# A two-level Strassen MLP: the 15-sum form, sums chained in PSUM, and a second level in the first matmul

What was changed: the outer products of a tuned MLP kernel go over from the 18-sum to the 15-sum form of a seven-product scheme (two ways to write it, with 18 or 15 sums of blocks around the seven products), their sums are chained in PSUM, the operands over g are made in place, products 2 and 3 of the first matmul get a second level, and x is cast before it is transposed.

## The chip, the cores and the metric

The kernel runs on one core of one Trainium2 chip. The metric is the device time of one launch in microseconds (us), the median of several runs. A profile of one execution is taken beside the timed runs; its "span", from the first to the last instruction, is some 1.8 us shorter than that execution's time. The granted TensorE clock, as a share of full speed, is given where it matters.

PE is TensorE's matmul side, PEld its weight loads, DVE is VectorE, ACT is ScalarE, POOL is GpSimd, SP is SyncE, whose queue (SPq) issues most loads.

## The reference

```python
x: (8, 1024, 1024)   w1: (1024, 4096)   w2: (4096, 1024)      # float32, normal draws
h = x @ w1
h = 0.5 * h * (1 + np.tanh(np.sqrt(2 / np.pi) * (h + 0.044715 * h ** 3)))
out = (h @ w2).astype(np.float32)
```

The kernel computes in float16 with float32 sums.

## The kernel before

The 8192 rows of x are worked on in eight row blocks of 1024 rows, numbered 0 to 7 here (`sb` in the code). For each one, "matmul 1" makes g = gelu(x w1) and "matmul 2" makes g w2. Both see their operands as 2 x 2 blocks and make seven block products instead of eight. Matmul 2 of row blocks 2 to 7 does so on two levels: each of the seven products is again seven smaller ones, of 256 columns. Matmul 1 has one level only, with matmuls of 512 columns. In row blocks 0 and 1 the operands made from w1 and w2 are made for the first time and stored in DRAM; later row blocks load them.

Matmul 1 before, for one chunk `c` of 128 rows of g (cut):

```python
pb, qb = psum(), psum()
product(pb, w, 4, True, False)          # four matmuls of 512 columns
v = temp()
nc.scalar.copy(out=v, in_=pb)
product(qb, w, 5, True, False)
u = temp()
tt(u, v, qb, SUB)                       # tt: a VectorE tensor_tensor
...
rb = psum()
product(rb, w, 1, True, False)
s = temp()
tt(s, u, rb, ADD)
product(pb, w, 2, False, True)
gelu("21", c, pb)
s2 = temp()
tt(s2, s, pb, SUB)
product(qb, w, 3, False, False)
gelu("12", c, qb)
product(rb, w, 7, False, True)
c11 = temp()
tt(c11, u, rb, ADD)
gelu("11", c, c11)
late = (c, w, qb, s2)                   # product 6 and g22: in the next chunk
```

That is five VectorE sums of 128x512 per chunk. In matmul 2 of row block 0 the first results leave PSUM through VectorE:

```python
for q, ps in product2(g, 4, pieces(4), pb, True, True):
    u[q] = temp()
    nc.vector.tensor_copy(out=u[q], in_=ps)
bring(("22",), late_copy, True)         # load w2's blocks and cast them on ScalarE
bring(("12",), late_copy, True)
```

The inner sums of w2 that row blocks 2 to 7 load are made on the way, some of them in matmul 1 of row blocks 1 and 2, half of those on GpSimd (`split_in_m1`, cut).

## Time and profile before

The median was 1513.1 us of 3 runs (1511.92 to 1513.27). What matters of the profile:

| | us |
|---|---|
| span | 1510.3 |
| start and matmul 1 of row block 0, until matmul 2 begins | 119.16 |
| matmul 2 of row block 0 | 96.70 |
| matmul 1 of row block 1 | 98.65 |
| matmul 2 of row block 1 | 96.69 |
| row blocks 2 to 7, to the end | 1099.1 |
| of that, one matmul 1 / one matmul 2 | 96.69 / 85.59 |

The page of the kernel before, its first line and the busy times of the engines:

```profile
span 1510.3 us, 24616 instructions
## 1 busy us (share of the span) xinstructions
PE 1499.5 (99%) x9278; PEld 908.6 (60%) x9278; DVE 1136.3 (75%) x1442; ACT 527.8 (35%) x958; POOL 409.4 (27%) x368
```

PE is busy 99% of the span, so a step that does not shorten PE's work, or its few gaps, gains nothing. The chain of work that ended last, kernel before (start in us, length in us, what):

```profile
411.37 96.82 PE ps L358 x448
508.19 85.59 PE ps L738 x784
593.77 96.69 PE ps L358 x448
```

One block of matmuls follows another with nothing between them. 96.69 us over 448 matmuls is 215.8 ns for 512 columns, and 85.59 us over 784 is 109.2 ns for 256. The four largest waits of PE in the whole run of the kernel before (waiting engine, line and tile; releaser; us in total, times, longest us):

```profile
PE ps L358 <- DVE tmp L144: 2.6, 4, 1.6
PE ps L358 <- DVE u L144: 1.5, 1, 1.5
PE ps L287 <- DVE warm L895: 1.2, 1, 1.2
PE ps L738 <- DVE u L144: 0.4, 1, 0.4
```

And the busy time of the engines in one later matmul 1 and one later matmul 2, kernel before:

```profile
core 0: us, PE busy (x) PEld busy (x) DVE busy (x) ACT busy (x) POOL busy (x), PEclk, DMA share, GB/s
593.61:690.30 96.69, 96.69 (x450) 43.83 (x448) 55.80 (x80) 46.29 (x79) 35.48 (x21) 1.00 0.84 253
508.20:593.80 85.60, 85.60 (x785) 76.65 (x784) 81.35 (x95) 18.26 (x43) 10.90 (x12) 1.00 1.00 337
```

VectorE, with 81.35 of 85.60 us, is nearly full in matmul 2, although PE waits for it there only once in the whole run, for 0.4 us.

### The profile page before, as it was taken

What the parts mean: (1) busy time and instruction counts of PE and PEld (TensorE: products, weight loads), DVE (VectorE), ACT (ScalarE), POOL (GpSimd) and SP (SyncE); (2) the same over time, 40 slices, a digit from 0 to 9 for tenths busy, and PEclk for the clock granted to TensorE, in tenths of its full rate; (3) what the DMA queues carried; (4) which work ended last, traced back from release to release, by engine and by line L of the source; (5) the groups of instructions that cost most, each with busy time, mean ns of one, the idle gap of its engine ahead of it and who ended that gap; (6) DMA issues with size and microseconds to landing.
All of it is one profiled execution on the core that took longest, in us unless ns stands there. A gap on an engine that the chain in (4) does not pass through costs nothing.

```text
span 1510.3 us, 24616 instructions
## 1 busy us (share of the span) xinstructions
PE 1499.5 (99%) x9278; PEld 908.6 (60%) x9278; DVE 1136.3 (75%) x1442; ACT 527.8 (35%) x958; POOL 409.4 (27%) x368
## 2 busy tenths in 40 slices
PE   9999999999999999999999999999999999999998
PEld 4444444444444687447864488644885458844687
DVE  5876868877755799558985589755996568965798
ACT  6655014420044322443234422344224442244321
POOL 1242022211379302170121601234112431105101
PEclk9999999999999999999999999999999999999999
DMA  9999877995899899968998899987999879994697
GB/s 319 341 342 363 241 269 279 337 357 176 318 372 251 302 317 347 311 164 313 318 320 282 201 327 323 302 252 204 358 315 310 237 220 337 312 365 147 211 324 240
DMA packets 235191, 438.92 MB, mean 291 GB/s; under 512 B 79552, under 2 KB 86720, under 8 KB 234176
## 3 DMA queue, kind: packets, MB, share of 16 engines
q1 hardware_dynamic: 205056, 337.71, 65.5%
q0 software_dynamic: 30016, 99.63, 23.0%
q8 instruction: 73, 1.20, 0.3%
q14 instruction: 46, 0.38, 0.1%
HBM read 334.50 MB, written 117.44 MB: 299 GB/s over the span
## 4 chain that ended last, share of the span: by engine, by line
PE 83%; DMA 1%; DVE 0%; issue 0%; DVEq 0%
PE ps L358 43%; PE ps L738 34%; PE ps L789 6%; DMA u<-raw_d 1%; DVE u L144 0%; DVE tmp L144 0%; DVEq L144 0%
## 5 line engine op out<-in xcount | busy, mean ns | idle before, releaser
L358 PE MATMUL ps<-u 128*128 128x512 f16 x3584 | 777.1, 379 | 4.3 <-DVE tmp L144 2.6
L358 PEld LDWEIGHTS <-u 128*128 128x128 f16 x3584 | 350.5, 98 | 428.6 <-issue 7.0
L144 DVE TENSOR_TENSOR tmp<-tmp,ps 128x512 f32<-128x512 f32 x528 | 362.2, 687 | 282.2 <-ACT tmp L422 109.7
L738 PE MATMUL ps<-u,gc 128*128 128x256 f16 x2688 | 300.4, 273 | 0.4 <-DVE u L144 0.4
L738 PEld LDWEIGHTS <-gc 128*128 128x128 f16 x2688 | 263.0, 98 | 31.2 <-issue 0.6
L368 ACT ACTIVATE g<-tmp 128x512 f16<-128x512 f32 x256 | 161.0, 631 | 287.2 <-DVE tmp L144 287.0
L144 DVE TENSOR_TENSOR u<-u 128x512 f32<-128x512 f32 (+3 forms) x278 | 239.5, 897 | 15.3 <-ACT u L313 12.4
L160 ACT COPY u<-ps 128x512 f32<-128x512 f32 x164 | 96.2, 586 | 390.2 <-PE ps L738 390.2
L492 POOL DMA_DIRECT2D out_dram<-u x80 | 76.3, 1090 | 556.6 <-DVE u L144 275.5
L368 ACT ACTIVATE g<-ps 128x512 f16<-128x512 f32 x256 | 152.1, 596 | 100.4 <-PE ps L358 100.3
L144 DVE TENSOR_TENSOR u<-u,ps 128x512 f32<-128x512 f32 x188 | 128.4, 683 | 32.7 <-PE ps L789 17.2
L789 PE MATMUL ps<-u,gc 128*128 128x512 f16 x640 | 138.8, 379 | 0.0
L738 PE MATMUL ps<-u,g 128*128 128x256 f16 x1152 | 132.6, 273 | 0.0
L738 PEld LDWEIGHTS <-g 128*128 128x128 f16 x1152 | 112.7, 98 | 14.3
L468 POOL TENSOR_TENSOR u<-g,g 128x2048 f16<-128x2048 f16 x24 | 97.0, 4064 | 44.7 <-ACT g L368 44.7
L789 PEld LDWEIGHTS <-gc 128*128 128x128 f16 x640 | 62.6, 98 | 75.5
L738 PE MATMUL ps<-u 128*128 128x256 f16 x864 | 99.2, 273 | 0.0
L144 DVE TENSOR_TENSOR tmp<-ps,tmp 128x512 f32<-128x512 f32 x128 | 88.4, 690 | 13.1 <-PE ps L358 8.5
L738 PEld LDWEIGHTS <-u 128*128 128x128 f16 x864 | 84.6, 98 | 9.8
L422 ACT COPY tmp<-ps 128x512 f32<-128x512 f32 x128 | 73.0, 570 | 36.1 <-PE ps L358 36.1
L144 DVE TENSOR_TENSOR u<-g,g 128x2048 f16<-128x2048 f16 x48 | 57.9, 1222 | 9.0 <-PE ps L738 9.0
L144 DVE TENSOR_TENSOR gc<-g,gc 128x2048 f16<-128x2048 f16 x48 | 58.6, 1220 | 1.0 <-ACT g L368 1.0
(43 smaller groups left out, 664.5 us busy)
## 6 DMA issues: line engine op xcount, KB each, us to landing
u<-w_d SPq DMA_DIRECT2D x420, 256.0 KB, 6.7
u<-in_d SPq DMA_DIRECT2D x168, 512.0 KB, 7.4
u<-raw_d SPq DMA_DIRECT2D x168, 256.0 KB, 6.4
out_dram<-u POOLq DMA_DIRECT2D x80, 512.0 KB, 10.5
gc<-in_w_dram SPq DMA_DIRECT2D x48, 512.0 KB, 5.6
w_d<-u POOLq DMA_DIRECT2D x36, 512.0 KB, 6.0
raw_d<-u SPq DMA_DIRECT2D x32, 512.0 KB, 10.7
u<-raw_d SPq DMA_DIRECT2D x32, 512.0 KB, 11.5
```

What stands on the lines that cost most here:

```text
L144: i = nc.vector.tensor_tensor(out=out, in0=in0, in1=in1, op=op)
L160: tc.keep_in_program_order(nc.scalar.copy(out=out, in_=in_))
L358: nc.tensor.matmul(bank, lhsT=ops[:, k, :], rhs=xs[m][:, k, :], start=(first and k == 0), stop=(k == KH - 1), skip_group_check=not first,)
L368: gelu_last[0] = nc.scalar.activation(out=g[b][:, c, :], in_=src, func=GELU)
L422: nc.scalar.copy(out=v, in_=pb)
L468: nc.gpsimd.tensor_tensor(out=early[m][b], in0=gu, in1=gv, op=SUB)
L492: return nc.gpsimd.dma_start(out=rows, in_=src, **kw)
L738: tc.keep_in_program_order(nc.tensor.matmul(bank[:, i * OH // 2:(i + 1) * OH // 2], lhsT=t[:, c, i * P:(i + 1) * P], rhs=self.y[j][:, c, : ...
L789: i = nc.tensor.matmul(pair(bank), lhsT=a[:, c, :], rhs=chunks(pieces[c // QC])[:, :, c % QC, :], start=(first and c == 0), stop=(c == NI ...
```

## The change

The intent is less work on TensorE: with a second level in products 2 and 3 of matmul 1, fourteen matmuls of 256 columns stand for eight of 512. The 15-sum form and the chains in PSUM are there to pay for the VectorE work that this adds. In the new form product 1 goes into a bank, is copied out, product 6 is added on top of it in the same bank and copied out, then product 7, then product 4: the bank holds in turn the partial sums that the four results need. For an inner level the same is done in one half bank, `chain`, which VectorE must read between the parts.

The core of the diff (cuts are marked with `...`):

```diff
-B_TERMS = {1: ("11", SUB, "22"), 2: ("11", None, None), 3: ("12", ADD, "22"), ...
-A_TERMS = {...
+W_TERM = {1: "11", 2: "21", 3: "22"}
+W_SUM = {5: ("12", SUB, "11"), 6: ("22", SUB, 5), 7: ("22", SUB, "12"), 4: ("21", SUB, 6)}
+S_TERM = {1: "11", 2: "12", 4: "22"}
+S_SUM = {7: ("11", SUB, "21"), 6: ("22", SUB, 7), 5: ("21", ADD, "22"), 3: ("12", SUB, 6)}
+INNER_1 = (2, 3)
+SPLIT_IN_M1 = (1, 2, 3)
+FILL = (                      # which small job follows which product (m, q) of matmul 2,
+    slots("""10:g60;11:g61;12:g62;13:g63          # row blocks 0 and 1
+    ;20:g50 w50 w51;21:g51 w52;22:w53 g52;23:g53
+    ;50:w60 w61;51:w62 w63;52:g30 g31;53:g32 g33
+    ;60:w70 w71;61:w72 w73;62:w40 w41;63:w42 w43
+    ;30:x5;31:x7;32:x6;33:x3
+    ;70:q5;71:q6;72:q7;73:q4
+    ;40:i2;41:i3"""...), ...
+FILL_2 = slots("""...          # the same for row blocks 2 to 7
+    ;31:z11 z12;32:z21 z22;33:v11 v12;34:v21 v22;36:n6;37:n3 i3"""...)
 ...
+        def steps(m, source, cs, banks, acc):          # matmul 1, a product with inner level
+            ...
+            part(1, chain, True)                       # two matmuls of 256 columns
+            part(2, banks[0][:, left], fresh)
+            yield add(acc[0][:, left], chain)          # VectorE
+            part(6, chain)
+            part(3, banks[0][:, right])
+            yield add(acc[0][:, right], chain)
+            part(7, chain)
+            part(5, c5, fresh)
+            part(4, banks[1][:, left])
+            add(acc[1][:, left], chain)
+            add(acc[1][:, right], chain)
+            add(acc[0][:, right], c5)
+            ...
+        for j in range(NI // 2):                       # pairs of chunks
+            ...
+            for h in range(2):
+                product(banks_a[h], source, 1, cs[h], True)
+                act_copy(a[h], banks_a[h])
+            ...                       # product 2, with product 4 of the pair before in between
+            for h in range(2):
+                add(a[h], banks_b[h])
+            ...                       # products 5, 6, 3 and 7
 ...
-        for q, ps in product2(g, 4, pieces(4), pb, True, True):
-            u[q] = temp()
-            nc.vector.tensor_copy(out=u[q], in_=ps)
+        def post(m, q, bank):                          # matmul 2, row blocks 0 and 1
+            if m in (1, 5, 6):
+                t = {1: a, 5: p5, 6: t6}[m]
+                t[q] = temp()
+                act_copy(t[q], bank)                   # ScalarE, in program order
+            ...
 ...
-            if m in (2, 5):
-                tt(t[n], in0, in1, op, True)
-            else:
-                nc.gpsimd.tensor_tensor(out=t[n], in0=in0, in1=in1, op=op)
+            tt(t[n], in0, in1, op, True)               # inner sums of w2 in matmul 1
```

In the job lists, `g` makes an operand over g, `w` one over w2, `p` an inner sum of w2, `x` or `n` one over the next x, `q` one over w1, and `i2`, `i3` the inner sums for products 2 and 3 (of w1 in row block 0, of x later). In `FILL_2`, `z` and `v` add results to one another.

## The prediction

> **What bounds the kernel now.** TensorE: busy 1499.5 of 1510.3 us at a granted clock of 1.0 (page). The chain of waits is one block of matmuls after another: in each of the six later row blocks 96.69 us for matmul 1 (448 of 512 columns, 215.8 ns each) and 85.59 us for matmul 2 (784 of 256 columns, 109.2 ns each). [...] The rest: the first product starts at 19.56 us (timeline), later gaps sum to about 7 us, the tail after the last matmul is 4.4 us.
>
> **TensorE.** In row blocks 2 to 7, products 2 and 3 of matmul 1 get a second level: per pair of chunks 8 matmuls of 512 columns (1.726 us) become 14 of 256 (1.529 us). Saved: 0.198 us x 2 products x 8 pairs x 6 row blocks = 19.0 us, all on the critical path. Nothing else changes its count of products. I expect about 93.5 us per later matmul 1.
>
> **VectorE.** Back to back, 128x512 f32 sums start 0.60 us apart, 128x2048 f16 sums 1.135 us. Later matmul 1: from 5 PSUM sums per chunk to 3, plus 11 sums of 256 columns per pair and one f16 difference. [...] Busy share rises from 57% (windows) to 75 to 80%. Later matmul 2: 46 f16 and 48 f32 sums become 43 and 52 with 8 small ones, an estimate of 83 us against 81 measured, of 85.6: nearly full. In matmul 1 the chained bank must be read between two parts of a second-level product, with one product (0.86 us) as cover. By hand the steady pair just fits; I allow 0.05 to 0.3 us of PE idle per pair and about 1 us per change of stage: 6 to 12 us in all.
>
> **DMA.** Stored inner sums of w1 add 25 MB in all; two accumulating stores less per row block come off (12 MB). Matmul 1 has spare DMA time (share 0.5 to 0.65 in its second half): no lasting stall.
>
> **Start.** Transposes become f16, and products 1 and 2 need only half of x and the left half of w1's columns: first product near 14 us. But product 5 needs all of x and both column halves, 6.3 MB, there at about 21 to 22 us at the measured 0.33 MB/us. The 3.5 us of early work about fills what is won: gain 0 to 3 us.
>
> **Sum.** 1513 - 19 - 1.5 + about 1 net of new and removed stalls = 1493.5 us, range 1484 to 1506. Chances: faster by over 2% 0.08, within 2% 0.89, slower 0.03.
>
> **What would show it.** Right: PE blocks of 93.5 to 95 us in later matmul 1, 85.6 to 87 in matmul 2; 1344 matmuls of 256 columns more and 768 of 512 fewer; VectorE at 75% or more in matmul 1, over 95% in matmul 2. Wrong: PE waiting on VectorE at the chained bank in every pair (0.4 us each would eat the gain); PE waiting on stored w1 sums; a gap over 5 us after the first two products; gaps where products 6 and 3 of matmul 2, drained by VectorE instead of ScalarE, hold a bank.
>
> **What would make it wrong.** VectorE's queue is in order: one sum that waits for data delays all behind it, and at 97% load it can't catch up. A start that overlaps better would bring it near 1485.

## The result and the profile after

The changed kernel took 1512.09 us (median of 4 runs, 1508.69 to 1514.19) against 1512.51 for the kernel before (4 runs). The ratio is 0.9995, with a 95% interval of 0.9974 to 1.0017: no difference. Ratios here are the mean time of one kernel's runs over that of the other's of the same rounds, so not quite the ratio of the medians.

The predicted saving did not come, and the page of the changed kernel says at once that it was not for want of less work:

```profile
span 1511.7 us, 26283 instructions
## 1 busy us (share of the span) xinstructions
PE 1483.2 (98%) x9839; PEld 959.9 (63%) x9839; DVE 1164.9 (77%) x1820; ACT 616.1 (41%) x1157; POOL 228.1 (15%) x315
```

PE is busy 16.3 us less than before, and the span is 1.4 us longer: the difference is idle time. Stage by stage:

| us | before | changed | difference |
|---|---|---|---|
| start and matmul 1 of row block 0 | 119.16 | 117.29 | -1.9 |
| matmul 2 of row block 0 | 96.70 | 102.93 | +6.2 |
| matmul 1 of row block 1 | 98.65 | 103.31 | +4.7 |
| matmul 2 of row block 1 | 96.69 | 96.69 | 0 |
| row blocks 2 to 7, to the end | 1099.1 | 1091.5 | -7.6 |

(Each boundary is the start of the first matmul of the next stage in the timeline of PE.) So there are three places to explain: two stages of the first two row blocks, and row blocks 2 to 7, which gained 7.6 us instead of 19. The three largest waits of PE, changed kernel:

```profile
PE ps L397 <- DVE tmp L120: 12.1, 14, 3.3
PE ps L898 <- DVE u L120: 3.8, 3, 1.8
PE ps L397 <- DVE u L120: 3.1, 2, 2.7
```

All three are waits for VectorE. But VectorE is not the place where the time is lost; it is where three different delays surface.

**Place 1: matmul 2 of row block 0.** The timeline of all engines there, changed kernel (start in us, length in us, what; in brackets the idle time just before and what ended it):

```profile
132.49 1.05 ACT L657 CAST u<-u 128x1024 f16<-128x1024 f32 x1 [5.22 <-DMA u<-in_w_dram]
...
141.76 1.04 ACT L657 CAST u<-u 128x1024 f16<-128x1024 f32 x1 [0.19 <-DMA u<-in_w_dram]
142.71 2.04 ACT L136 COPY tmp<-ps 128x512 f32<-128x512 f32 x4
143.32 0.69 DVE L120 TENSOR_TENSOR tmp<-tmp,ps 128x512 f32<-128x512 f32 x1 [19.79 <-ACT tmp L136]
...
146.34 2.15 PE L898 MATMUL ps<-u,g 128*128 128x512 f16 x8 [1.26 <-DVE u L120]
...
150.34 1.02 PE L898 MATMUL ps<-u,g 128*128 128x512 f16 x4 [1.84 <-DVE u L120]
```

The four copies of product 1 (L136) could have run from about 121 us on, as each quarter of the product was ready (a run below copies the first at 120.82). They ran together at 142.71, behind ScalarE's casts of w2 (L657), which waited for their loads. VectorE's next sum needs such a copy, so VectorE idled for 19.79 us, and the sums for product 5, behind it in its queue, came late.

**Place 2: matmul 1 of row block 1.** VectorE in the changed kernel around the longest wait of PE:

```profile
276.26 1.23 DVE L120 TENSOR_TENSOR u<-u 128x2048 f16<-128x2048 f16 x1 [2.04 <-DMA u<-raw_d]
278.90 1.23 DVE L120 TENSOR_TENSOR u<-u 128x2048 f16<-128x2048 f16 x1 [1.42 <-DMA u<-raw_d]
283.27 0.69 DVE L120 TENSOR_TENSOR gc<-gc 128x1024 f16<-128x1024 f16 x1 [3.14 <-DMA in_d<-gc]
283.88 1.28 DVE L120 TENSOR_TENSOR tmp<-tmp,ps 128x512 f32<-128x512 f32 x2
```

Sums over w1 (`u<-u`) wait for loads, and an inner sum of w2 (`gc<-gc`) waits for a store that must free one of four small buffers. The sums that empty PSUM (`tmp<-tmp,ps`) stand behind them, and PE stands for 3.33 us until 284.62. Then it pays once more. The windows of the changed kernel around that wait (the column after POOL's busy time is the granted clock):

```profile
280.00:284.60 4.60, 1.28 (x6) 0.49 (x5) 1.46 (x4) 0.00 (x1) 0.88 (x2) 1.00 1.01 405
284.60:288.70 4.10, 4.08 (x12) 1.53 (x12) 3.56 (x6) 4.10 (x8) 1.53 (x4) 0.58 0.44 168
288.70:300.00 11.30, 11.30 (x54) 5.17 (x53) 10.56 (x19) 6.14 (x13) 3.74 (x9) 1.00 0.95 333
```

For 4.1 us after the wait the mean clock is 0.58, and 12 matmuls begin where 19 would at full speed. In narrower windows of this run the clock is 1.00 from 284.60 to 285.20 us, 0.50 from 285.20 to 288.40 and 1.00 from 288.70 on; in the clock records of its packed trace the stretch at 0.50 is 3.41 us long, which gives that mean.

**Place 3: the first pair of chunks of row blocks 3 to 7.** VectorE and then PE in the changed kernel, at the change from matmul 2 of row block 2 to matmul 1 of row block 3 (from the timelines of the two engines):

```profile
599.66 1.22 DVE L120 TENSOR_TENSOR u<-u 128x2048 f16<-128x2048 f16 x1
600.79 0.68 DVE L120 TENSOR_TENSOR u<-u,ps 128x512 f32<-128x512 f32 x1
601.39 2.81 DVE L120 TENSOR_TENSOR u<-u 128x2048 f16<-128x2048 f16 x5
604.11 0.42 DVE L120 TENSOR_TENSOR tmp<-tmp,ps 128x256 f32<-128x256 f32 x1
```

```profile
600.22 3.19 PE L397 MATMUL ps<-u 128*128 128x512 f16 x16
604.58 4.28 PE L397 MATMUL ps<-u 128*128 128x256 f16 x26 [1.17 <-DVE tmp L120]
609.15 86.83 PE L397 MATMUL ps<-u 128*128 128x256 f16 x502 [0.29 <-DVE tmp L120]
```

(A merged row carries the shape of its first instruction; 5 sums are one of 2048 and four of 512.) PE is in matmul 1 from 600.22 us on, while VectorE still makes the last jobs of matmul 2: `n3` and the four sums of `i3`, 2.81 us. The first read of the chained bank, the row at 604.11, comes after them, and PE waits for it. The same two waits come back in each row block from 3 to 7, to the hundredth of a microsecond or so. Matmul 1 there takes 95.60 us (600.22 to 695.82); its 320 matmuls of 512 columns and 224 of 256, at 215.8 and 109.2 ns, need 93.52. Of the 2.08 us between, the waits and restarts in the first pair are 1.79 us. The rest is small: the packed trace, read matmul by matmul, has one late start of 44 to 47 ns in each of the seven other pairs, always where a matmul of 256 columns begins 52 or 53 ns after the end of VectorE's read of the chained bank. `prof` lists idle time from 150 ns on, so these don't show in its views.

The windows of the changed kernel over most of that matmul 2 and over that matmul 1:

```profile
549.46:600.22 50.76, 50.76 (x467) 45.41 (x465) 47.60 (x61) 6.02 (x15) 5.44 (x6) 1.00 0.86 276
600.22:695.82 95.60, 94.13 (x546) 53.23 (x544) 68.89 (x147) 60.12 (x109) 10.18 (x15) 1.00 0.95 285
```

VectorE is busy 72% of matmul 1 and 94% of the matmul 2 before it: busy, but not over its capacity. That its order is what costs is tested below.

### The profile page after: what moved, and what is told of

The parts are those of the page before. It is cut to its first block, busy times and chain, and to the rows that moved or that the text cites. A ratio compares the mean times of both kernels' runs of the same rounds, so it can differ in the third digit from the quotient of the medians.

```text
span 1511.7 us, 26283 instructions
## 1 busy us (share of the span) xinstructions
PE 1483.2 (98%) x9839; PEld 959.9 (63%) x9839; DVE 1164.9 (77%) x1820; ACT 616.1 (41%) x1157; POOL 228.1 (15%) x315
## 3 DMA queue, kind: packets, MB, share of 16 engines
q8 instruction: 77, 1.26, 0.3%
## 4 chain that ended last, share of the span: by engine, by line
PE 83%; DVE 7%; DMA 5%; issue 3%; POOL 1%; ACT 0%; SPq 0%; DVEq 0%; POOLq 0%
PE ps L397 42%; PE ps L857 30%; PE ps L898 11%; DVE u L120 6%; DMA u<-in_w_dram 1%; DMA raw_d<-u 1%; DVE tmp L120 1%; DMA in_d<-gc 1%; DMA u<-in_x_dram 1%; DMA gc<-raw_d 1%; DVE gc L120 0%; DMA out_dram<-tmp 0%; POOL in_d L806 0%; SPq L133 0%; POOL w_d L214 0%
## 5 line engine op out<-in xcount | busy, mean ns | idle before, releaser
L397 PE MATMUL ps<-u 128*128 128x512 f16 (+1 forms) x4160 | 764.1, 346 | 16.4 <-DVE tmp L120 12.1
L120 DVE TENSOR_TENSOR tmp<-tmp,ps 128x256 f32<-128x256 f32 (+1 forms) x936 | 454.0, 533 | 274.8 <-PE ps L397 162.0
L136 ACT COPY tmp<-ps 128x512 f32<-128x512 f32 x416 | 235.1, 581 | 324.3 <-PE ps L397 160.9
L410 ACT ACTIVATE g<-tmp 128x512 f16<-128x512 f32 x384 | 241.7, 633 | 175.9 <-DVE tmp L120 175.7
L857 PE MATMUL ps<-u,g 128*128 128x256 f16 x2016 | 227.9, 273 | 0.0
L136 ACT COPY u<-ps 128x512 f32<-128x512 f32 (+1 forms) x136 | 78.8, 586 | 346.1 <-PE ps L857 341.5
L857 PEld LDWEIGHTS <-g 128*128 128x128 f16 x2016 | 197.3, 98 | 24.7
L898 PE MATMUL ps<-u,g 128*128 128x512 f16 x768 | 168.7, 382 | 3.9 <-DVE u L120 3.8
L898 PEld LDWEIGHTS <-g 128*128 128x128 f16 x768 | 75.5, 98 | 96.5 <-issue 5.7
L120 DVE TENSOR_TENSOR g<-g,g 128x2048 f16<-128x2048 f16 (+1 forms) x136 | 131.0, 986 | 1.6 <-ACT g L410 1.6
L120 DVE TENSOR_TENSOR gc<-g 128x2048 f16<-128x2048 f16 x78 | 95.2, 1221 | 0.0
```

The costliest lines, as they stand in the source:

```text
L120: i = nc.vector.tensor_tensor(out=out, in0=in0, in1=in1, op=op)
L136: tc.keep_in_program_order(nc.scalar.copy(out=out, in_=in_))
L397: tc.keep_in_program_order(nc.tensor.matmul(bank, lhsT=w, rhs=x, start=first and k == 0, stop=k == n - 1, skip_group_check=not first,))
L410: gelu_last[0] = nc.scalar.activation(out=g[b][:, c, :], in_=src, func=GELU)
L857: tc.keep_in_program_order(nc.tensor.matmul(bank[:, i * OH // 2:(i + 1) * OH // 2], lhsT=t[:, c, i * P:(i + 1) * P], rhs=self.y[j][:, c, : ...
L898: tc.keep_in_program_order(nc.tensor.matmul(pair(bank), lhsT=a[:, c, :], rhs=chunks(pieces[c // QC])[:, :, c % QC, :], start=(first and c ...
```

## The experiments

Theory A: VectorE, ScalarE and the SP queue each work in order (in place 1 ScalarE's copies, which could have run from about 121 us on, ran at 142.71 behind its casts, and VectorE idled for 19.79 us with the sums for product 5 behind the one that waited; for the SP queue `splits_on_pool` below shows it, with loads of w1 behind two loads that took 17.83 us to be issued), and in the three places a job that waits for a load, a store or a turn stands ahead of one that PE needs. Rivals (theory B in the texts, different in each) are that the DMA engines are too full, that the small matmuls cost more than counted, or that the wait is the plain latency of the chain between PE and VectorE. All kernels gave correct results. The first four ran beside the kernel before at 1512.19 us, the next four beside it at 1511.69, the last three at 1512.13.

### one_level: the change without the second level in matmul 1

```diff
-INNER_1 = (2, 3)
+INNER_1 = ()
-HALF_ORDER = (1, 2, "s2", 5, 6, 3, "s3", 7, 4)
+HALF_ORDER = (1, 2, 5, 6, 3, 7, 4)
```

and without the jobs `i2` and `i3`.

> The changed kernel without the second level of products 2 and 3 in matmul 1 (all products of matmul 1 are four matmuls of 512 columns; the inner sums of x and of w1 are not made, stored or loaded). Theory A (the second level does save 19 us of TensorE time, but about 12 us of it come back as waits at the first pair of chunks of each later row block, where VectorE is behind): later matmul 1 takes 96.7 to 97.0 us instead of 95.6 and has no wait of over 0.3 us, so the total rises by about 6 us, to about 1518 us. Theory B (the matmuls of 256 columns themselves or their data cost more than the trace of before said, and the rest is unaffected): the total stays within 3 us or falls. The losses in row blocks 0 and 1 (6 us in matmul 2 of row block 0, 4 to 5 us in matmul 1 of row block 1) should stay, the second one a little smaller, as 2.8 us of inner sums per group of w1 columns are gone there.

Measured: 1514.28 us (ratio to the kernel before 1.0013, 0.9998 to 1.0028). Later matmul 1 takes 96.7 us and PE waits nowhere from row block 2 on, as theory A said; but the total rose by 2 us, not by 6, and by its total alone the run would have spoken for theory B ("within 3 us"). The miss is in row block 1: its matmul 1 fell from 103.31 to 96.69 us with no wait, where I had expected it to be only "a little smaller". So the second level's jobs also bring about place 2. All in all the second level was worth some 2 us in the changed kernel, which is not clear of the scatter (the intervals of the two kernels overlap).

### copy_on_vector: product 1 of row block 0 copied by VectorE

```diff
+                if sb == 0 and m == 1:
+                    tc.keep_in_program_order(nc.vector.tensor_copy(out=t[q], in_=bank))
+                else:
+                    act_copy(t[q], bank)
-                act_copy(t[q], bank)
```

> The changed kernel with one edit: in matmul 2 of row block 0 the four copies of product 1 out of PSUM are made by VectorE instead of ScalarE. Theory A (head of the queue: on ScalarE those copies stand behind sixteen casts of w2 that wait for their loads until 142 us, so VectorE stands still for 20 us and then makes the sums for product 5 too late): matmul 2 of row block 0 falls from 102.9 us to 97 to 98 us, VectorE takes up its sums near 131 us instead of 143, and the total falls by 5 to 6 us, to about 1506. Theory B (w2 arrives too late, because the DMA engines are full at 0.91): PE waits as long as before for the same sums, and the total stays within 1.5 us.

Measured: 1507.35 us (0.9965, 0.9951 to 0.9980), 4.7 us under the changed kernel. The timeline of PE in this run (the first 192 matmuls, from 117.16 us on, left out):

```profile
158.60 13.98 PE L901 MATMUL ps<-u,gc 128*128 128x512 f16 x64
172.42 41.60 PE L901 MATMUL ps<-u,g 128*128 128x512 f16 x192
213.86 36.42 PE L397 MATMUL ps<-u 128*128 128x512 f16 x168
```

Matmul 2 of row block 0, from 117.16 us on, is 96.70 us without a gap. The casts and the loads of w2 are what they were; the rival, loads that come too late, falls. Place 1 is shown: it was the ScalarE queue's order.

### splits_on_pool: inner sums of w2 on GpSimd in row block 1

```diff
-            tt(t[n], in0, in1, op, True)
+            nc.gpsimd.tensor_tensor(out=t[n], in0=in0, in1=in1, op=op)
```

> The changed kernel with one edit: in matmul 1 of row block 1 the inner sums of w2 for products 1, 2 and 3 are made by GpSimd instead of VectorE. Theory A (VectorE's queue stands still behind those sums, which wait for four small buffers that are freed by stores and filled by loads; PE waits for VectorE's drains, and its clock falls): matmul 1 of row block 1 falls from 103.3 us to 97 to 99 us, the 3.3 us wait at 284 us is gone, and the total falls by 4 to 6 us. Theory B (the loads of w1 or the DMA rate hold matmul 1 up): the waits stay, on sums of w1, and the total stays within 1.5 us.

Measured: 1549.29 us (1.0254, 1.0233 to 1.0275), 37 us slower than the changed kernel. Neither theory said so. The SP queue of this run shows the reason:

```profile
216.65 17.83 SPq L795 DMA_DIRECT2D gc<-raw_d  x2
234.59 3.19 SPq L169 DMA_DIRECT2D u<-raw_d  x4
```

Two loads into the small buffers take 17.83 us to be issued, because GpSimd, at 2.13 us a sum (VectorE in the changed kernel: 0.69), frees those buffers slowly (the queue's waits for GpSimd's sums at these loads come to 54.0 us between 195 and 260 us). The loads of w1 stand behind them in the same queue; VectorE waited 28.7 us for such a load, and PE 17.5 us for VectorE, now in matmul 2 of row block 0, where the scheduler had moved some of the work. So this run does not test the theory for place 2. It shows that a slower engine that holds buffers can stop everything through the load queue.

### inner_later: the last job moved behind the first sums of matmul 1

```diff
-...;36:n6;37:n3 i3"""
+...;36:n6;37:n3"""
```

(the kernel then makes these sums after the first pair's sums of product 2).

> The changed kernel with one job moved: the four inner sums of x for product 3 of the next row block are no longer made in the last step of matmul 2, but after the sums of the first pair of chunks in matmul 1. Theory A (at each change of row block VectorE is some 2 us behind, and the first read of the chained bank waits for it): the 1.2 us wait in the first pair is gone in row blocks 3 to 7, later matmul 1 falls from 95.6 to about 94.3 us, and the total falls by 5 to 7 us. Theory B (the wait there is the latency of the chain from PE to VectorE and back, as the first pair has only one product as cover): the waits stay, and the total stays within 1.5 us.

Measured: 1512.48 us (1.0001, 0.9983 to 1.0020): nothing. PE in this run, at the same place:

```profile
600.06 7.31 PE L397 MATMUL ps<-u 128*128 128x512 f16 x42
609.12 2.12 PE L397 MATMUL ps<-u 128*128 128x256 f16 x14 [1.76 <-DMA u<-raw_d]
```

The first wait is gone and the second has grown from 0.29 to 1.76 us (the releaser named is the one that came last by the profile; VectorE's read of the second chain, at 608.66, ends just before). The 1.55 us of inner sums were only put ahead of the next read that PE needs. My expectation was wrong: moving a job within the busy stretch is not taking it out.

### inner_on_pool: the same sums on GpSimd

```diff
-                tt(operand(j), operand(u), operand(v), op, True)
+                if pool:                                   # product 3, row blocks 3 to 7
+                    tc.keep_in_program_order(
+                        nc.gpsimd.tensor_tensor(out=operand(j), in0=operand(u), in1=operand(v), op=op)
+                    )
+                else:
+                    tt(operand(j), operand(u), operand(v), op, True)
```

> The changed kernel with one edit: in the later row blocks the four inner sums of x for product 3 (the last job of matmul 2) are made by GpSimd instead of VectorE. The run that only moved them behind the first sums of matmul 1 lost the 1.2 us wait but got one of 1.76 us at the next read of a chained bank. Theory A (VectorE has too much to do around the change of row block: whatever is taken off its queue there comes off the waits): the first wait is gone and the second is no longer than the 0.3 us of the changed kernel, later matmul 1 falls from 95.6 to 94.0 to 94.4 us, the total by 5 to 7 us. Theory B (the wait is the latency of the chain; the order of the jobs does not matter): one wait of about 1.2 to 1.8 us stays, the total within 1.5 us.

Measured: 1504.54 us (0.9954, 0.9938 to 0.9971), 7.5 us under the changed kernel. In the trace the first wait is gone and the second is 0.39 us; the row blocks follow each other at 180.1 us instead of 181.3, which is 6 us of the gain (five changes of row block). The spans of the two profiled runs differ by more, 9.8 us; there the rest lies in matmul 2 of row block 0, which took 98.7 us in this profile against 102.9 in the changed kernel's, with no edit there. The cost of place 1 is not the same in every profile: in those of kernels that leave it alone it was between 2 and 6 us (`splits_on_pool`, disturbed by its load queue, left out), which may also be why the changed kernel's runs scatter more (1508.69 to 1514.19) than those of the kernel before. GpSimd is slower at these sums, 4.60 us for the four (trace of `first_pair`) against 1.55 on VectorE (trace of `inner_later`), but it was idle: at row block 3 it had made them at 603.56 us, and PE went on with product 3 at 604.11.

### first_pair: and the first pair's sums reordered

```diff
-            for h in range(2):
-                add(a[h], banks_b[h])
+            hold = sb > 1 and j == 0
+            if not hold:
+                fold()                     # the same two sums
 ...
                     next(three)            # first read of product 3's chained bank
+                    if hold:
+                        fold()
                     six(1)
```

> As the run with those inner sums on GpSimd, and in the first pair of the later row blocks the two sums of 512 columns of product 2 come after the first read of product 3's chained bank instead of ahead of it. Theory A: the remaining wait of 0.3 us (0.45 us with the end of the last matmul counted) goes too, and later matmul 1 falls to 93.5 to 93.9 us; total 7 to 11 us under the changed kernel. Theory B: nothing more than the run without this reordering.

Measured: 1503.88 us (0.9946, 0.9932 to 0.9961), 8.2 us under the changed kernel. In its profile 3.8 us of the gain lie in matmul 2 of row block 0, without an edit there, and the gain over inner_on_pool is within the scatter, so the trace has to speak for this edit. All waits of PE over 0.15 us in row blocks 2 to 7 are gone; the row blocks follow at 179.8 us and matmul 1 takes 94.05 us, a little more than the 93.5 to 93.9 expected. Place 3 is shown: the cost was the amount and the order of VectorE's work at the change of row block, and not the latency of the chain. That latency has a price too, but a small one: the 44 to 47 ns in each of the seven other pairs.

### splits_earlier: inner sums of w2 for products 1 to 3 made in row block 0

With the copies on VectorE, and:

```diff
-SPLIT_IN_M1 = (1, 2, 3)
+SPLIT_IN_M1 = ()
-    slots("""10:g60;11:g61;12:g62;13:g63
+    slots("""10:g60 p15;11:g61 p16;12:g62 p17;13:g63 p14
 ...
-    ;30:x5;31:x7;32:x6;33:x3
+    ;30:x5 p35;31:x7 p36;32:x6 p37;33:x3 p34
```

(the four of product 2 go into other slots in between).

> As the run with the copies on VectorE, and the inner sums of w2 for products 1 to 3 are made in matmul 2 of row block 0, where w2 is in SBUF anyway, instead of in matmul 1 of row block 1, which then has neither their loads nor their stores nor their four small buffers. Theory A (VectorE's queue in matmul 1 of row block 1 stands still behind loads and stores of those sums): matmul 1 of row block 1 falls from 104 to 96.7 to 98 us, matmul 2 of row block 0 stays at 96.7 to 98, and the total is 5 to 7 us under the run with the copies alone, near 1501 us. Theory B (it is the inner sums of w1, or the loads of w1, that hold VectorE up there; the run with one level had no wait there): matmul 1 of row block 1 stays over 100 us.

Measured: 1508.31 us (0.9976, 0.9961 to 0.9991), no gain over the copies alone, where 1501 had been expected. Matmul 1 of row block 1 did fall, from 103.98 to 96.69 us, without a wait. But matmul 2 of row block 0 rose from 96.70 to 103.77 us. PE there, this run:

```profile
172.44 27.79 PE L901 MATMUL ps<-u,g 128*128 128x512 f16 x128
205.28 15.84 PE L901 MATMUL ps<-u,g 128*128 128x512 f16 x64 [5.04 <-DVE tmp L120]
220.96 96.86 PE L397 MATMUL ps<-u 128*128 128x512 f16 x448
```

The wait had moved: the last transpose of x is issued at 193.4 us instead of 182.5 (most likely because of the added stores), and VectorE stands for 8.21 us at the job `x7` ahead of the sums that PE needs. For place 2 the two runs say this: taking away either the inner sums of w2 with their buffers (here) or the inner sums of w1 (one_level) clears it. Neither by itself is the cause. VectorE's queue in that stage could bear one of the two, and the second level put both into it. One rival is left for place 2: the DMA engines had a share of 1.01 to 1.04 from 266 to 284.6 us of the changed kernel, and both runs also took transfers out of that stage, so that full DMA engines are not excluded there.

### mended: all of these together

Copies on VectorE, splits in row block 0, `i3` on GpSimd, the first pair reordered.

> All of these mends together: copies of product 1 on VectorE in row block 0, inner sums of w2 for products 1 to 3 in row block 0, inner sums of x for product 3 on GpSimd, and the first pair reordered. If the losses are separate (theory A) they add: 1512 minus 5, minus 6, minus 9, so about 1492 us, 1.3% under the kernel before, with later matmul 1 at 93.5 to 94 us. If the waits only move from one place to the next (theory B), the total stays over 1502 us.

Measured: 1499.14 us (0.9921, 0.9906 to 0.9935). That lies between the two theories (1492 or over 1502): the gains that the copies and the first pair had alone, 4.7 and 8.2 us, add up, and the splits brought none on top; 4.58 us of wait in matmul 2 of row block 0 remain, the moved one.

### mended_later: the jobs that need the transposed x put later

```diff
-    ;30:x5 p35;31:x7 p36;32:x6 p37;33:x3 p34
-    ;70:q5;71:q6;72:q7;73:q4
-    ;40:i2;41:i3"""
+    ;30:p35;31:p36;32:p37;33:x5 p34
+    ;72:x7;73:x6
+    ;40:x3 q5;41:q6 q7;42:q4 i2;43:i3"""
```

> As the run with all mends, with the jobs of matmul 2 of row block 0 that need the transposed x put later: in the run before VectorE stood 8.7 us at such a job, as the transposes landed until 195 us, and PE waited 4.6 us for drains queued behind it. Theory A (head of the queue, once more): matmul 2 of row block 0 falls from 102.7 to 96.7 to 98 us, and the total from 1499 to about 1493 us. Theory B (DMA, busy 0.98 in that stage, is what holds it up): the wait turns up later, in product 4 or at the start of the next matmul 1, and the total stays over 1497 us.

Measured: 1495.35 us (0.9885, 0.9872 to 0.9899). Matmul 2 of row block 0 takes 97.90 us and matmul 1 of row block 1 96.69. The largest waits of PE in this run, summed by place:

```profile
PE ps L402 <- DVE u L120: 5.3, 3, 2.6
PE ps L402 <- ACT u L197: 1.5, 1, 1.5
PE ps L305 <- DVE warm L998: 1.2, 1, 1.2
PE ps L344 <- DVE tmp L340: 1.1, 2, 0.7
PE ps L913 <- DVE u L120: 0.9, 2, 0.7
```

All but the last row are in the first 29 us. The DMA rival falls for this wait: the same bytes move in the whole run (443.21 MB), and the wait is gone.

### mended_clock: the wait at the start filled with matmuls on zeros

```diff
             for _ in two:
                 pass
+            if start is not None and j == 0:
+                keep_clock(start.idle, 12)
```

> As that run, and twelve matmuls on zeros fill the 2.65 us for which PE waits for the first sums of product 5 at the start (the granted clock is 0.74 between 20 and 25 us in the changed kernel). If the clock costs what it seems to, the 16 matmuls after the wait take 3.5 us instead of 5.3 and the total falls by 1 to 2 us; if VectorE's sums are what holds the start up, PE waits longer for the next sums instead and nothing is won.

Measured: 1494.49 us (0.9881, 0.9866 to 0.9896), against 1495.35 without it. That is within the scatter. The profiled run without the filling had a clock of 1.0 after its wait this time, so the two traces do not test the clock. They do show that matmul 1 of row block 0 ends at the same time in both, 118.2 us: VectorE's sums set the start.

### mended_one_level: the second level by itself, with the waits gone

> As the run with all mends and the later jobs, without the second level of products 2 and 3 of matmul 1. It measures the second level by itself, where its waits are gone. Theory A (its saving is the 19.0 us that the count of matmuls says, and only the waits ate it in the changed kernel): later matmul 1 takes 96.7 to 96.9 us and the total is 16 to 19 us higher, near 1510 us. Theory B (the second level has a cost of its own): less than 12 us higher.

(the edit of one_level, on mended_later). Measured: 1510.10 us (0.9985, 0.9972 to 0.9997), 14.8 us above mended_later, between theory A's 16 to 19 and theory B's 12. Its row blocks follow each other at 182.38 us, mended_later's at 179.79: 2.6 us per row block where the count of matmuls says 3.17. So in the changed kernel the second level was worth 2 us, and with its waits removed it is worth about 15. The missing 0.5 us per row block lie in matmul 1 (94.05 against 93.52), in no wait that `prof` lists. Read matmul by matmul, the trace of mended_later has them: 0.24 us of late starts in the first pair and 41 to 47 ns in each of the other seven, 0.56 us together, nearly all where PE takes up a second-level product again after VectorE's read of its chained bank. So the second level has a small cost of its own, the latency of the chain.

## Why the prediction was wrong

The text expected 1493.5 us, with a range of 1484 to 1506; 1512.09 us were measured.

- **What bounds the kernel: right.** PE was busy 99% before and 98% after, and the last mends gained only where they removed idle time of PE.
- **The saving on TensorE, 19.0 us: nearly right.** The counts came out as predicted, 768 matmuls of 512 columns fewer and 1344 of 256 more, at the predicted times each. By itself the second level measured 14.8 us of it (mended_one_level).
- **The start, 0 to 3 us: right.** Product 1 began at 11.36 us (predicted near 14), product 5 at 21.76 (predicted 21 to 22), and matmul 1 of row block 0 ended 1.9 us earlier. A gap of 2.65 us after the first two products was there, as the text allowed for.
- **VectorE's load: right in size.** Its busy share was 72% in matmul 1 (predicted 75 to 80) and 95.8% in a whole matmul 2 (82.06 us of 85.70; predicted over 95). The sums of 256 columns lasted 0.42 us.
- **The step that failed is the last term of the sum, "about 1 net of new and removed stalls".** It measured about 22 us: 11.2 in row blocks 2 to 7 (2.08 in each of five matmul 1, 0.75 in the first), 6.2 in matmul 2 of row block 0 (of the profiled run), 6.6 in matmul 1 of row block 1, less 2.0 that the kernel before lost in the latter. For row blocks 2 to 7 the text had 6 to 12 us, so the range held it, but it expected them in every pair of chunks, at 0.05 to 0.3 us, and about 1 us per change of stage. The pairs cost 0.05 us each, the low end, and the change of row block 1.8 us. To come to "about 1 net", the sum seems to have set most of the kernel before's 7 us of gaps against this; outside the start only 2.0 us of them went. For row blocks 0 and 1 it named no time at all. There I had compared VectorE's work with the length of the stage and found room, and had not asked what each job in its queue waits for. The last paragraph named the danger ("one sum that waits for data delays all behind it") and then gave it no time. The trace of the kernel before has such a case: at 309.54 us a sum had waited 1.03 us for its load, and the one behind it began (310.68) 2.81 us after ScalarE's copy did (307.87), where 0.60 us is usual (600.25 to 600.85).
- **Two further things were not in the sum.** ScalarE's queue can also hold back VectorE (place 1, 19.79 us). And two of the stops cost more than their length: after the 3.33 us wait 4.1 us ran at a clock of 0.58, and after the waits of place 1, three of 1.26, 1.84 and 0.71 us close together, the clock was 0.71 from 150 to 155 us. From these means the lost time is an estimated 1.7 and 1.5 us, and it is part of the 22. The 2.65 us wait at the start was followed by a clock of 0.74 from 20 to 25 us in the changed kernel, and by one of 1.00 in mended_later.

The arithmetic closes: -19.0 on TensorE, -1.9 at the start and +22.0 of stalls make +1.1; the spans differ by +1.4.

What stays open: how place 2 splits between loads that came late (with full DMA engines or not) and buffers that were freed late, since one run removed both; and what VectorE's slow sums at the start cost. Six of the first twelve sums of 128x1024 there took 1.10 to 1.52 us, the other six 0.68 to 0.69. The trace ties the slow ones to GpSimd: in the whole run 12 of 136 such sums took over 0.8 us (1.10 to 1.54), and each of the 12 overlaps GpSimd's casts by at least 0.55 us, while 117 of the 124 others overlap none. No run took GpSimd's casts away, so this is not tested.

## What to carry to other kernels

A busy share tells whether an engine can do the work, not whether it does it in time (VectorE was busy for 72% of a later matmul 1 that lost 2.08 us, nearly all of it to waits for VectorE): for each in-order queue, list what every job waits for, and what stands behind it that the bound engine needs. A saving on the bound engine is real only as far as no such job lies between; here 19 us were saved and as much was lost to a few jobs at the change of stage, and moving those jobs, without taking any work away from TensorE, gave 1.2% over the kernel before. When a job is moved, look where its wait went: two of the mends here only carried it to the next place.
